# Squares off GpSimd, compress weights loaded early, and a few moves in the first stage of a one-core decoder layer

## The chip, the cores and the metric

The kernel runs on one core of a Trainium2 chip. The metric is the time of one execution in device microseconds (us); three runs of the kernel before gave 1188.03, 1190.80 and 1195.89 us, so the median is 1190.8 us. The engines are named as the profile names them: PE (matrix multiply), PEld (its weight load, which overlaps), DVE (vector), ACT (scalar activations), POOL (GpSimd) and SP (it only issues DMA here).

## The reference, cut to what matters

One transformer layer on 256 tokens of width 2048, in float32:

```python
h = rmsnorm(x, norm_attn)                  # y = x * rsqrt(mean(x*x) + eps) * g
proj = h @ w_in                            # columns split among three mixers
o_a = dilated_mixer(pA, tbl_a)             # three windows, weighted by softmax shares
o_b = moba_mixer(q, k, v, tbl_b)
o_c = nsa_mixer(q_c, kv_c, g_c, cmp_w1, cmp_w2, cmp_pe, tbl_c)
x = x + concatenate([o_a, o_b, o_c]) @ w_out
h = rmsnorm(x, norm_mlp)
x = x + conv_ffn(h, w_up, conv_w, conv_b, w_down)
return rmsnorm(x, norm_final)
```

Two pieces matter here. `rmsnorm` needs the sum of squares of each token over all 2048 features. `nsa_mixer` compresses blocks of 32 keys (and values) by a small two-layer network, `gelu(blocks @ cmp_w1) @ cmp_w2`, and weighs its three branches by gates `g_c`, a sigmoid of 36 projected columns.

## The kernel before, in words

**Layout.** Activations lie feature by feature: `x` is 16 tiles (kt = 0 to 15) of 128 features by 256 tokens. Every weight tile comes from HBM as float32 into one of four `raw` buffers (loads issued by SP, in program order while the first stage is written, L663). ACT rounds it into `wh` (L122) and DVE computes the rest `wl = raw - wh` (L124); there are five buffers of each. `x` is split in the same way into `xx` (ACT L174, DVE L175). A product is then two PE instructions: `wl` against the high part of `xx` (L186, 256 columns) and `wh` against both parts (L182, 512 columns). `Weights.get` runs three jobs ahead.

**First units.** `first_units` works on six units of 128 output columns (`ckv0` to `ckv5`) at once, while x arrives. Its blocks go by kt: four small ones for kt 0 and 1, two for kt 2 and 3, then three groups of three (kt 4 to 7, 8 to 11, 12 to 15); a block of a group is one load of 512 KB and 8 products, a group 24 products. After each piece of x lands, `x_load` splits it, and POOL squares it and adds the squares one tile at a time into `ssq` (L240, L242). `Rms` then sums `ssq` over the partitions by a matmul with ones (L146), which stands in PE's order among the products of the last group. `evac` scales the six units and writes the compressed branch's keys and values into `K2`.

**The group `c`, then the rest.** `tm_group("c")` multiplies 420 columns (L385 to L387, 96 matmuls), among them the gate columns. `compress` loads its 2 MB of weights `w1t` in four DMAs (L414), into the space that held the squares (`sqx`, tag `oo`), runs 32 matmuls of 49 columns (L422, two records each in the trace), a gelu, and three small matmuls with `w2t` (L445 to L447). At the end of the group the gates are turned end to end by a matmul with `flip` (L402). Then come the query units `cq0` to `cq5`, the other heads, all attention, and the output projection in two passes. The second pass (L701 to L710) adds to each tile of x, splits it again for the feed-forward part, and POOL squares and adds it (L168, L170) into `ssq2`; two units `up` of the feed-forward part are multiplied meanwhile, and the second norm's matmul (L146) stands in PE's order among them. The up and down projections, about 60% of the time, follow.

The order on PE, ACT, DVE and POOL is set when the kernel is built, by a scheduler that simulates the engines; only SP's order in the first units is the program's own.

Of the kernel before, what the change touches and what calls it, by code (L numbers as in the profile page):

```python
# [11 lines left out]
F32 = mybir.dt.float32  # L12
F32R = mybir.dt.float32r
AF = mybir.ActivationFunctionType
# [3 lines left out]
P = 128  # L18
S = 256
# [70 lines left out]
def trunk(ctx, tc, xT, wfm, wtm, wout, wup, wdown, w1, w2, pe, relT, convp, onehot, maskc, cmask, vbmask, out):  # L90
# [19 lines left out]
    def warm_sqrt(src):  # L110
        A.activation(warm, src, AF.Sqrt)

    warm_sqrt(ones[:, :1])

    def split_w(src, n, before=None):
        if before:
            before()
        raw = wp.tile([P, CHUNK], F32, name="raw", bufs=RAW_BUFS)
        dst = raw[:, :n]
        DMA(dst if len(src.shape) == 2 else dst.rearrange("p (u c) -> p u c", u=src.shape[1]), src)  # L120
        wh = wp.tile([P, CHUNK], F32R, name="wh")
        A.copy(wh[:, :n], raw[:, :n])  # L122
        wl = wp.tile([P, CHUNK], F32R, name="wl")
        V.tensor_tensor(wl[:, :n], raw[:, :n], wh[:, :n].bitcast(F32), ALU.subtract)  # L124
        return wh, wl
# [13 lines left out]
    class Rms:  # L139
# [17 lines left out]
        def spread(self, keep=True):  # L157
# [5 lines left out]
            rb = cp.tile([P, S], F32, name="rbc")  # L163
            V.tensor_copy(rb, ps[:, S:])
            return rb

    def add_squares(ssq, o, tmp):
        G.tensor_tensor(tmp, x[:, o, :], x[:, o, :], ALU.mult)  # L168
        if o:
            G.tensor_tensor(ssq, ssq, tmp, ALU.add)  # L170

    def split_x(gi, kts, xx):
        for kt in kts:
# [33 lines left out]
    with tc.tile_pool(name="sc", bufs=2, space=bass.MemoryType.PSUM) as scp, \  # L207
# [20 lines left out]
        order.insert(len(order) - 8, ("t", "b"))  # L228
        ssq = cp.tile([P, S], F32, name="ssq2")

        sqx = ap.tile([P, 12, S], F32, name="sqx", tag="oo")

        def x_load(*cuts):
            def go():
                for a, b in zip(cuts, cuts[1:]):
                    i, j = GX * (a > 0) + a * S, GX + b * S
                    DMA(gx[:, i:j], xT[:, i:j])
                    split_x(0, range(a, b), xx)
                    c = a % 12
                    G.tensor_tensor(sqx[:, c:c + b - a, :], x[:, a:b, :], x[:, a:b, :], ALU.mult)  # L240
                    for o in range(max(a, 1), b):
                        G.tensor_tensor(ssq, ssq if o > 1 else sqx[:, 0, :], sqx[:, o % 12, :], ALU.add)  # L242
            return go


# [3 lines left out]
            blocks += [(0, 2, 4 * g, 4, cuts), (2, 2, 4 * g, 4, None), (4, 2, 4 * g, 4, None)]  # L249
        for u, nu, kt, nk, cuts in blocks:  # L250
            src = wfm[u:u + nu, :, kt * P:(kt + nk) * P].rearrange("u p c -> p u c")
            jobs.append((src[:, 0, :] if nu == 1 else src, nu * nk * P, x_load(*cuts) if cuts else None))
        for kind, name in order:
            (fm_jobs if kind == "f" else tm_jobs)(name)
        for o in range(NK):
# [13 lines left out]


        flip = ap.tile([P, P], F32, name="flip")
        V.tensor_copy(flip, ident[:, ::-1])
        relt = ap.tile([NB, NB], F32, name="relt")
        G.dma_start(relt, relT)
        oneh = rp.tile([NB, 384], F32, name="sb")
# [13 lines left out]
        table = dr.tile([NB, 384], F32, name="table")  # L289

        def biases():
            ps = opp.tile([P, 512], F32, name="o")
            T.matmul(ps[:NB, :384], relt, oneh, start=True, stop=True)
            rs = ap.tile([NB, 384], F32, name="rs", tag="oo")
            V.scalar_tensor_tensor(rs, ps[:NB, :384], -1.0, mc, ALU.mult, ALU.add)
            G.dma_start(table, rs)

# [61 lines left out]
        def first_units():  # L359

            pss = [pool.tile([P, 512], F32, name=n) for pool, n in
                   ((mm, "mm"), (opp, "o"), (scp, "sc"), (scp, "sc"), (mm, "mm"), (ptp, "pt"))]
            for u, nu, kt, nk, _ in blocks:
                if (u, kt) == (0, 12):
                    clear()
                    n = Rms([ssq])
                w = wq.get()
                for j in range(nu):
                    products(pss[u + j], tuple(t[:, nk * P * j:nk * P * (j + 1)] for t in w), nk, kt, xx, kt == 0, kt == 12)
                    if kt == 12:  # L370
                        if u + j == 0:
                            norm(n)
                        evac(f"ckv{u + j}", pss[u + j])

        def tm_group(name):
            n = len(_TM[name])
            pss = [mm.tile([P, 512], F32, name="mm") for _ in range(2)]
            for c in range(8):
                wh, wl = wq.get()
                for i in range(2):  # L380
                    kt = 2 * c + i
                    a, b = wh[:, i * n:(i + 1) * n], wl[:, i * n:(i + 1) * n]
                    for tt in range(2):
                        ts = slice(tt * P, tt * P + P)
                        T.matmul(pss[tt][:, :n], xx[:, kt, 0, ts], a, start=kt == 0, stop=False)  # L385
                        T.matmul(pss[tt][:, :n], xx[:, kt, 1, ts], a, start=False, stop=False)  # L386
                        T.matmul(pss[tt][:, :n], xx[:, kt, 0, ts], b, start=False, stop=kt == NK - 1)  # L387
                yield
            nv = n - n % P
            v = vt[name] = ap.tile([P, 2, nv], F32, name=f"v_{name}", tag=f"v{name}")  # L390
            rt = st["rt"]
            if name == "c":
                ge = st["gate"] = ap.tile([P, 2, 36], F32, name="gate")
            for tt in range(2):
                A.activation(v[:, tt, :], pss[tt][:, :nv], AF.Copy, scale=rt[:, tt, 0:1])
                if name == "c":
                    A.activation(ge[:, tt, :], pss[tt][:, nv:n], AF.Exp, scale=rt[:, tt, 1:2])
            if name == "c":
                V.tensor_scalar_add(ge, ge, 1.0)
                V.reciprocal(ge, ge)  # L400
                ps = mm.tile([P, 512], F32, name="mm")
                T.matmul(ps[:, :72], flip, ge.rearrange("p t g -> p (t g)"), start=True, stop=True)  # L402
                V.tensor_copy(ge.rearrange("p t g -> p (t g)"), ps[:, :72])

        oparts = {}
        oo = []
# [2 lines left out]
        cmp = {}  # L409

        def compress():
            w1t = ap.tile([P, 4, 8 * P], F32, name="w1t", tag="oo")
            for i in range(4):
                DMA(w1t[:, i, :], w1[i // 2, :, i % 2 * 1024:i % 2 * 1024 + 1024])  # L414
                yield
            hps = ptp.tile([P, 512], F32, name="pt")
            for i in range(2):
                k2 = K2[i][:, :, 16:256].rearrange("p h (b l) -> p h b l", l=16)
# [40 lines left out]
            yield  # L459

        def cmp_attention():
            sm = rp.tile([P, 2, 12, 16], F32, name="sb")
            for tt in range(2):
                sps = scp.tile([P, 512], F32, name="sc")
# [194 lines left out]
        def drain():  # L659
            while side:  # L660
                step()

        with tc.manual_schedule(engines={mybir.EngineType.SP}):  # L663
            first_units()
        biases()
# [35 lines left out]
        for o in range(NK):  # L701
            if o % 2 == 0:
                w = wq.get()
            ps = mm.tile([P, 512], F32, name="mm")
            for i in range(4):
                a, b = (t[:, (o % 2 * 4 + i) * P:(o % 2 * 4 + i + 1) * P] for t in w)
                product_in_one(ps, a, b, oparts[6 + i], i == 0, i == 3)
            add_to_x(o, ps, 1)
            split_x(1, [o], xx)
            add_squares(ssq2, o, rp.tile([P, S], F32, name="sq", bufs=1) if o else ssq2)  # L710


    jobs = []
# [160 lines left out]
```

## Time and profile before

| | us |
|---|---|
| median of 3 runs | 1190.8 |
| the profiled execution | 1189.61 |
| its span in the trace | 1187.9 |
| PE busy in it | 1163.6 |
| DVE, ACT, POOL busy | 861.6, 671.3, 83.9 |

An engine's busy time says how much of the span it worked; what matters for the end is where PE, busy for nearly all of it, stood still or ran slowly, and which engine or transfer ended that. "PEclk" is the clock that PE was granted: 1.00 is the upper level of 2.4 GHz, 0.50 the lower of 1.2 GHz, and a stretch in between is a mean of both.

### The profile page before, as it was taken

The numbers are of one execution on the slowest core, as the hardware profiler recorded it, in microseconds if no ns is written. First come the engines' busy times: TensorE is split into PE (matmuls) and PEld (weight loads), VectorE is DVE, ScalarE is ACT, GpSimd is POOL, SyncE is SP. The second block draws the span as 40 slices with busy tenths as digits, with TensorE's granted clock in tenths as the row PEclk, the third lists the DMA queues.
The fourth block names the chain that finished last, engine by engine and source line by source line (L and its number), as shares of the span: only waits on it lengthen the run. The fifth ranks groups of instructions, "written<-read, shape, count | busy, mean of one in ns | idle before, by whom it ended". The sixth has DMA issues, their size and how long they took to land.

```text
span 1187.9 us, 18694 instructions
## 1 busy us (share of the span) xinstructions
PE 1163.6 (98%) x6874; PEld 1022.6 (86%) x6874; DVE 861.6 (73%) x1635; ACT 671.3 (57%) x1153; POOL 83.9 (7%) x105
## 2 busy tenths in 40 slices
PE   7999999999999999999999999999999999999996
PEld 6798888898888888888888888888888888888886
DVE  7857998767686797888888888888888655454453
ACT  6465697766774456565565565565565544444441
POOL 7400000100000190000000000000000000000000
PEclk9989999999999999999999999999999999999998
DMA  8565445566565645555555555555555656666661
GB/s 267 162 233 187 135 118 171 145 191 184 156 168 154 221 159 186 192 192 185 192 192 184 191 192 184 192 192 185 192 192 183 190 180 184 187 182 192 183 190 71
DMA packets 66795, 214.91 MB, mean 181 GB/s; under 512 B 7584, under 2 KB 10416, under 8 KB 66704
## 3 DMA queue, kind: packets, MB, share of 16 engines
q1 hardware_dynamic: 64896, 209.19, 55.2%
q0 software_dynamic: 1808, 4.53, 2.1%
q8 instruction: 54, 0.88, 0.3%
q14 instruction: 37, 0.30, 0.1%
HBM read 211.55 MB, written 2.15 MB: 180 GB/s over the span
## 4 chain that ended last, share of the span: by engine, by line
PE 91%; POOL 5%; DMA 2%; DVE 1%; issue 0%; ACT 0%; SPq 0%; DVEq 0%; POOLq 0%
PE up L182 40%; PE up L186 20%; PE mm L182 12%; PE mm L186 6%; PE mm L387 2%; PE mm L385 2%; PE mm L386 2%; PE o L580 1%; POOL ssq L242 1%; POOL ssq L170 1%; POOL sq L168 1%; PE sc L509 1%; DMA w1t<-in_w_dram 1%; DMA raw<-in_wfm_dram 1%; PE pt L422 1%; PE pt L560 1%
## 5 line engine op out<-in xcount | busy, mean ns | idle before, releaser
L124 DVE TENSOR_TENSOR wl<-raw,wh 128x1024 fp32r<-128x1024 f32 (+4 forms) x411 | 485.0, 1182 | 200.2 <-ACT wh L122 190.9
L122 ACT CAST wh<-raw 128x1024 fp32r<-128x1024 f32 (+4 forms) x411 | 411.1, 1001 | 290.2 <-PE up L182 192.7
L182 PE MATMUL up<-xx,wh 128*128 128x512 f32 x1408 | 485.2, 394 | 0.0
L186 PE MATMUL up<-xx,wl 128*128 128x256 f32 x1408 | 380.2, 280 | 0.0
L182 PEld LDWEIGHTS up<-xx,wh 128*128 128x128 f32 x1408 | 258.6, 188 | 51.2
L186 PEld LDWEIGHTS up<-xx,wl 128*128 128x128 f32 x1408 | 266.0, 189 | 7.9
L182 PE MATMUL up<-aa,wh 128*128 128x512 f32 x660 | 230.7, 393 | 0.0
L186 PE MATMUL up<-aa,wl 128*128 128x256 f32 x660 | 184.1, 283 | 0.0
L182 PE MATMUL mm<-xx,wh 128*128 128x512 f32 x448 | 162.6, 403 | 4.4 <-ACT wh L122 4.4
L182 PEld LDWEIGHTS up<-aa,wh 128*128 128x128 f32 x660 | 123.0, 188 | 27.3
L186 PE MATMUL mm<-xx,wl 128*128 128x256 f32 x448 | 125.2, 289 | 3.1 <-DVE wl L124 3.1
L186 PEld LDWEIGHTS up<-aa,wl 128*128 128x128 f32 x660 | 124.1, 188 | 1.4
L203 ACT COPY low<-up 128x256 f32<-128x256 f32 x88 | 32.7, 372 | 129.9 <-PE up L182 127.3
L182 PEld LDWEIGHTS mm<-xx,wh 128*128 128x128 f32 x448 | 84.8, 192 | 20.6 <-ACT wh L122 4.4
L186 PEld LDWEIGHTS mm<-xx,wl 128*128 128x128 f32 x448 | 86.5, 193 | 7.0 <-DVE wl L124 4.4
L204 DVE TENSOR_TENSOR low<-up,low 128x256 f32<-128x256 f32 x88 | 37.4, 424 | 57.0 <-ACT low L203 57.0
L182 PE MATMUL mm<-oo,wh 128*128 128x512 f32 x192 | 67.8, 399 | 0.0
L738 ACT ACTIVATE acc<-u,cw 128x256 f32<-128x256 f32 x88 | 53.3, 606 | 3.0 <-DVE u L736 0.6
L186 PE MATMUL mm<-oo,wl 128*128 128x256 f32 x192 | 51.7, 282 | 0.0
L385 PE MATMUL mm<-wh,xx 128*128 128x384 f32 (+2 forms) x128 | 46.3, 363 | 0.0
L387 PE MATMUL mm<-wl,xx 128*128 128x384 f32 (+2 forms) x128 | 46.0, 361 | 0.0
L386 PE MATMUL mm<-wh,xx 128*128 128x384 f32 (+2 forms) x128 | 45.9, 359 | 0.0
(206 smaller groups left out, 1259.0 us busy)
## 6 DMA issues: line engine op xcount, KB each, us to landing
raw<-in_wup_dram SPq DMA_DIRECT2D x176, 512.0 KB, 4.3
raw<-in_wdown_dram SPq DMA_DIRECT2D x80, 512.0 KB, 3.7
raw<-in_wfm_dram SPq DMA_DIRECT2D x62, 512.0 KB, 4.0
raw<-in_wo_dram SPq DMA_DIRECT2D x32, 384.0 KB, 3.1
raw<-in_wtm_dram SPq DMA_DIRECT2D x16, 384.0 KB, 3.4
bias<-table POOLq DMA_DIRECT2D x32, 128.0 KB, 3.7
raw<-in_wtm_dram SPq DMA_DIRECT2D x8, 512.0 KB, 4.1
raw<-in_wo_dram SPq DMA_DIRECT2D x8, 512.0 KB, 4.3
```

The costliest lines, as they stand in the source:

```text
L122: A.copy(wh[:, :n], raw[:, :n])
L124: V.tensor_tensor(wl[:, :n], raw[:, :n], wh[:, :n].bitcast(F32), ALU.subtract)
L168: G.tensor_tensor(tmp, x[:, o, :], x[:, o, :], ALU.mult)
L170: G.tensor_tensor(ssq, ssq, tmp, ALU.add)
L182: T.matmul(ps, a, m.rearrange("p c s -> p (c s)"), start=start, stop=stop)
L186: T.matmul(ps[:, :S], b, m[:, 0, :], start=False, stop=False)
L203: A.copy(t, ps[:, S:])
L204: V.tensor_tensor(t, ps[:, :S], t, ALU.add)
L385: T.matmul(pss[tt][:, :n], xx[:, kt, 0, ts], a, start=kt == 0, stop=False)
L386: T.matmul(pss[tt][:, :n], xx[:, kt, 1, ts], a, start=False, stop=False)
L387: T.matmul(pss[tt][:, :n], xx[:, kt, 0, ts], b, start=False, stop=kt == NK - 1)
L738: A.activation(acc, u[:, 2:], AF.Identity, bias=cw[:, n, 3:4], scale=cw[:, n, 0:1])
```

## The change

The squares of the first norm go to ACT: the first four tiles straight into a four-tile sum `acc`, later pairs into a rotating `k` buffer, which DVE adds to `acc`; two more DVE additions fold `acc` into `ssq`. The squares of the second norm go to ACT in pairs of tiles too, and DVE adds the pairs. The four loads of `w1t` are issued by SP among those of the first units and of the group `c`. The first four weight loads go into spare `p` buffers instead of `raw` ones, the very first of them issued by ACT. Six matmuls of ones on ones run at the start. The gates are turned in `cmp_attention`, where they are used, not at the end of the group. `rs` moves to a `p` buffer, since `oo` now holds `w1t`.

```diff
+    idle = mm.tile([P, 512], F32, name="mm")
+    for _ in range(6):
+        T.matmul(idle[:, :P], ones, ones, start=True, stop=True)
-    def split_w(src, n, before=None):
+    def split_w(src, n, before=None, raw=None, load=DMA):
...
-        raw = wp.tile([P, CHUNK], F32, name="raw", bufs=RAW_BUFS)
+        raw = wp.tile([P, CHUNK], F32, name="raw", bufs=RAW_BUFS) if raw is None else raw()
...
-    def add_squares(ssq, o, tmp):
-        G.tensor_tensor(tmp, x[:, o, :], x[:, o, :], ALU.mult)
-        if o:
-            G.tensor_tensor(ssq, ssq, tmp, ALU.add)
...
-        sqx = ap.tile([P, 12, S], F32, name="sqx", tag="oo")
+        acc = ap.tile([P, 4, S], F32, name="acc", tag="vb")
+        def squares(a, b):
+            if b <= 4:
+                A.activation(acc[:, a:b, :], x[:, a:b, :], AF.Square)
+                return
+            for o in range(a, b, 2):
+                sq = rp.tile([P, 2, S], F32, name="k", bufs=KEY_BUFS)
+                A.activation(sq, x[:, o:o + 2, :], AF.Square)
+                part = acc[:, o % 4:o % 4 + 2, :]
+                V.tensor_tensor(part, part, sq, ALU.add)
...
                     split_x(0, range(a, b), xx)
-                    c = a % 12
-                    G.tensor_tensor(sqx[:, c:c + b - a, :], x[:, a:b, :], x[:, a:b, :], ALU.mult)
-                    for o in range(max(a, 1), b):
-                        G.tensor_tensor(ssq, ssq if o > 1 else sqx[:, 0, :], sqx[:, o % 12, :], ALU.add)
...
+                        + ((lambda: rp.tile([P, 384], F32, name="p", bufs=6), A.dma_start if (u, kt) == (0, 0) else DMA) if kt < 2 else ()))
...
-            rs = ap.tile([NB, 384], F32, name="rs", tag="oo")
+            rs = rp.tile([NB, 384], F32, name="p", bufs=6)
...
                 if (u, kt) == (0, 12):
                     clear()
+                    squares(8, 12)
+                    squares(12, 16)
+                    V.tensor_tensor(acc[:, :2, :], acc[:, :2, :], acc[:, 2:, :], ALU.add)
+                    V.tensor_tensor(ssq, acc[:, 0, :], acc[:, 1, :], ALU.add)
                     n = Rms([ssq])
+                if u == 0 and kt in (4, 8):
+                    for o in range(kt - 4, kt, 2):
+                        squares(o, o + 2)
                 w = wq.get()
+                if u == 4 and kt > 2:
+                    i = kt // 4 - 1
+                    for j in ((0,), (1,), (2, 3))[i]:
+                        DMA(w1t[:, j, :], w1[j // 2, :, j % 2 * 1024:j % 2 * 1024 + 1024])
...
-                ps = mm.tile([P, 512], F32, name="mm")
-                T.matmul(ps[:, :72], flip, ge.rearrange("p t g -> p (t g)"), start=True, stop=True)
-                V.tensor_copy(ge.rearrange("p t g -> p (t g)"), ps[:, :72])
...
         def compress():
-            w1t = ap.tile([P, 4, 8 * P], F32, name="w1t", tag="oo")
-            for i in range(4):
-                DMA(w1t[:, i, :], w1[i // 2, :, i % 2 * 1024:i % 2 * 1024 + 1024])
-                yield
...
         def cmp_attention():
+            ge = st["gate"].rearrange("p t g -> p (t g)")
+            ps = ptp.tile([P, 512], F32, name="pt")
+            T.matmul(ps[:, :72], flip, ge, start=True, stop=True)
+            V.tensor_copy(ge, ps[:, :72])
...
             split_x(1, [o], xx)
-            add_squares(ssq2, o, rp.tile([P, S], F32, name="sq", bufs=1) if o else ssq2)
+            if o % 2 == 1:
+                sq = rp.tile([P, 2, S], F32, name="k", bufs=KEY_BUFS)
+                A.activation(sq, x[:, o - 1:o + 1, :], AF.Square)
+                if o == 1:
+                    acc = sq
+                else:
+                    V.tensor_tensor(acc, acc, sq, ALU.add)
+        V.tensor_tensor(ssq2, acc[:, 0, :], acc[:, 1, :], ALU.add)
```

**The order, first place: PE in and behind the group `c`.** The rows are instructions in PE's order: line, operation, result and operands, columns, and how many follow alike. Before, all narrow matmuls of `compress` (the two rows with `w1t`) stand together behind the last matmul of the group, with the gates' matmul behind them and then the first products of `cq0`:

```order
L387 MATMUL mm<-wl,xx 128x420
L422 MATMUL pt<-k_0_111,w1t 128x49 x16
L422 MATMUL pt<-k_1_112,w1t 128x49 x16
L402 MATMUL mm<-gate,flip 128x72
L182 MATMUL mm<-xx,wh 128x512
```

Now, with new line numbers (L402 to L404 are the group's three matmuls, L432 the narrow ones):

```order
L404 MATMUL mm<-wl,xx 128x420
L432 MATMUL pt<-k_0_117,w1t 128x49 x16
L402 MATMUL mm<-wh,xx 128x420
L403 MATMUL mm<-wh,xx 128x420
L404 MATMUL mm<-wl,xx 128x420
L402 MATMUL mm<-wh,xx 128x420
L403 MATMUL mm<-wh,xx 128x420
L404 MATMUL mm<-wl,xx 128x420
L432 MATMUL pt<-k_1_118,w1t 128x49 x16
L402 MATMUL mm<-wh,xx 128x420
```

The narrow matmuls are now two bursts inside the group, 41 of the group's matmuls ahead of the first, 6 between them and 49 behind. The three matmuls with `w2t` follow directly on the group's last one; before, they stood behind the whole of `cq0`. The gates' matmul moved to just ahead of the first scores of `cmp_attention`.

**Second place: DVE at the end of the first units.** Before (L124 is `wl`, L204 the first unit's evacuation, L148 the first step behind the norm's matmul):

```order
L175 SCALAR_TENSOR_TENSOR xx<-gx,xx 128x256 x4
L124 TENSOR_TENSOR wl<-raw,wh 128x1024 x3
L124 TENSOR_TENSOR wl<-raw,wh 128x840 x2
L204 TENSOR_TENSOR low<-mm,low 128x256
L124 TENSOR_TENSOR wl<-raw,wh 128x840
L148 TENSOR_SCALAR var<-mm 128x2
```

Now:

```order
L173 SCALAR_TENSOR_TENSOR xx<-gx,xx 128x256 x2
L240 TENSOR_TENSOR acc<-acc,k 128x512
L173 SCALAR_TENSOR_TENSOR xx<-gx,xx 128x256 x2
L240 TENSOR_TENSOR acc<-acc,k 128x512
L127 TENSOR_TENSOR wl<-raw,wh 128x1024
L374 TENSOR_TENSOR acc<-acc 128x512
L127 TENSOR_TENSOR wl<-raw,wh 128x1024
L375 TENSOR_TENSOR ssq_99<-acc 128x256
L127 TENSOR_TENSOR wl<-raw,wh 128x1024
L127 TENSOR_TENSOR wl<-raw,wh 128x840 x2
```

Two additions of pairs, one fold of 512 columns and one of 256 now stand among the last group's `wl`; the sum is complete behind the second of its three `wl`. On PE the matmul with ones moved five products forward, to just behind the first product of the last group's second block.

**Third place: SP in the first units.** Before, from the load of the last tiles of x on, the four `w1t` loads stand behind the group `c` and three loads for `cq0` and `cq1`. Now:

```order
L123 DMA raw<-in_wfm_dram 128x2x512 x2
L384 DMA w1t<-in_w_dram 128x1024
L123 DMA raw<-in_wfm_dram 128x2x512
L246 DMA gx<-in_xT_dram 128x512 x2
L123 DMA raw<-in_wfm_dram 128x2x512 x2
L384 DMA w1t<-in_w_dram 128x1024
L123 DMA raw<-in_wfm_dram 128x2x512
L123 DMA raw<-in_wtm_dram 128x840 x2
L384 DMA w1t<-in_w_dram 128x1024 x2
L123 DMA raw<-in_wtm_dram 128x840 x6
```

One load stands in the second group of three blocks, one in the third, and two behind the second load of the group `c`.

At the second norm, 80 matmuls of the `up` units stand on PE ahead of the matmul with ones, where there were 64. On DVE, 9 of the 1024-column `wl` lie between the first addition to x of the second pass and `ssq2`. The copy that makes `flip` is written at another place, but keeps its place in DVE's order. No further table load appears on ACT.

## Rows read from the trace of the kernel before

**Rows 1.** The page, part 1: busy us, share of the span, instructions.

```profile
PE 1163.6 (98%) x6874; PEld 1022.6 (86%) x6874; DVE 861.6 (73%) x1635; ACT 671.3 (57%) x1153; POOL 83.9 (7%) x105
```

**Rows 2.** Waits of PE, whole span: us in total, times, longest.

```profile
PE mm L182 <- ACT wh L122: 4.4, 1, 4.4
PE mm L186 <- DVE wl L124: 3.1, 3, 1.4
```

**Rows 3.** Timeline of PE, parts: start us, us, instruction, idle before and its releaser.

```profile
4.96 0.63 PE L182 MATMUL o<-xx,wh 128*128 128x512 f32 x1
...
9.48 0.40 PE L182 MATMUL mm<-xx,wh 128*128 128x512 f32 x1
...
18.55 0.38 PE L186 MATMUL mm<-xx,wl 128*128 128x256 f32 x1 [1.08 <-DVE wl L124]
...
43.28 0.80 PE L146 MATMUL mm<-ones,ssq 128*128 128x1 f32 x4 [1.80 <-POOL ssq L242]
...
68.78 1.90 PE L422 MATMUL pt<-k,w1t 128*128 128x49 f32 x16
71.12 8.05 PE L422 MATMUL pt<-k,w1t 128*128 128x49 f32 x48 [0.45 <-DMA w1t<-in_w_dram]
...
446.05 0.81 PE L146 MATMUL mm<-ones,ssq 128*128 128x1 f32 x4 [2.71 <-POOL ssq L170]
```

**Rows 4.** Windows: length; busy (instructions) PE, PEld, DVE, ACT, POOL; PEclk, DMA, GB/s.

```profile
15.00:20.00 5.00, 3.92 (x23) 3.23 (x22) 4.77 (x8) 2.81 (x4) 1.48 (x2) 1.00 0.89 299
20.00:35.00 15.00, 14.95 (x86) 12.89 (x86) 15.00 (x13) 9.20 (x14) 14.61 (x13) 1.00 0.74 240
43.28:47.00 3.72, 3.72 (x14) 3.33 (x15) 2.31 (x9) 1.09 (x2) 0.00 (x0) 0.54 0.87 290
68.80:79.20 10.40, 9.96 (x66) 9.66 (x65) 4.05 (x8) 7.98 (x16) 0.00 (x0) 0.76 0.86 335
79.20:84.60 5.40, 5.40 (x19) 4.69 (x20) 2.88 (x10) 1.35 (x5) 0.00 (x0) 0.51 0.55 187
412.00:443.00 31.00, 31.00 (x236) 29.67 (x234) 29.05 (x42) 18.19 (x27) 28.48 (x29) 1.00 0.53 174
446.00:449.70 3.70, 3.65 (x14) 3.26 (x15) 2.36 (x7) 2.81 (x4) 0.17 (x3) 0.54 0.66 202
```

**Rows 5.** DVE groups by form, 20 to 43 us: count, busy, mean ns, idle.

```profile
L124 DVE TENSOR_TENSOR wl<-raw,wh 128x1024 fp32r<-128x1024 f32 x7 | 12.3, 1800 | 0.2 <-ACT wh L122 0.2
L175 DVE SCALAR_TENSOR_TENSOR xx<-gx,xx 128x256 fp32r<-128x256 f32 x8 | 7.8, 1033 | 0.0
```

**Rows 6.** The same, 412 to 443 us.

```profile
L124 DVE TENSOR_TENSOR wl<-raw,wh 128x1024 fp32r<-128x1024 f32 x10 | 14.1, 1420 | 1.5 <-ACT wh L122 1.5
L175 DVE SCALAR_TENSOR_TENSOR xx<-gx,xx 128x256 fp32r<-128x256 f32 x16 | 10.9, 698 | 0.3 <-ACT xx L174 0.3
L687 DVE TENSOR_TENSOR gx<-mm,gx 128x256 f32<-128x256 f32 x16 | 6.6, 412 | 0.2 <-PE mm L193 0.2
```

**Rows 7.** The same, 480 to 1150 us, where POOL has no work.

```profile
L124 DVE TENSOR_TENSOR wl<-raw,wh 128x1024 fp32r<-128x1024 f32 x232 | 284.2, 1225 | 118.8 <-ACT wh L122 111.6
L740 DVE SCALAR_TENSOR_TENSOR acc<-u,cw,acc 128x256 f32<-128x256 f32 x82 | 39.8, 485 | 2.9
...
L124 DVE TENSOR_TENSOR wl<-raw,wh 128x512 fp32r<-128x512 f32 x15 | 10.4, 692 | 10.5 <-ACT wh L122 10.5
```

**Rows 8.** ACT groups by form, whole span.

```profile
L122 ACT CAST wh<-raw 128x512 fp32r<-128x512 f32 x17 | 10.5, 620 | 27.0 <-PE up L182 25.2 <-PE up L192 1.7
```

**Rows 9.** Timeline of ACT: the sixth unit's evacuation and the copy of the hidden layer.

```profile
73.05 0.36 ACT L203 COPY low<-pt 128x256 f32<-128x256 f32 x1
...
80.09 0.23 ACT L429 COPY hT<-pt 128x98 f32<-128x98 f32 x1
```

**Rows 10.** Timeline of DVE: the last step ahead of the `w2t` matmuls.

```profile
82.33 0.39 DVE L442 COPY hr<-hT 128x60 f32<-128x60 f32 x3
```

**Rows 11.** DMA issues, whole span: count, KB each, median us to landing.

```profile
w1t<-in_w_dram SPq DMA_DIRECT2D x4, 512.0 KB, 9.2
```

## What the change was predicted to do

> **What bounds the kernel now.** I read the page's busy times first, then PE's waits, its timeline around them, the windows for the granted clock, and only then the engines that PE waited for. PE is busy for 1163.6 of 1187.9 us [rows 1]; 24 us of the span are left. So the change can win in two ways only: where PE stands still, and where it works at the lower clock. Both happen at three places.
>
> At 43.28 us PE has waited 1.80 us for the first norm's sum, which POOL makes, and then works 3.72 us at a mean clock of 0.54 [rows 3, 4]. From 68.78 us the narrow matmuls of the compressed branch run together; PE waits 0.45 us for `w1t` between them, the granted clock falls to a mean of 0.76 for 10.4 us, and the first products behind them still run at 0.51 for 5.4 us [rows 3, 4]. At 446.05 us PE has waited 2.71 us for the second norm's sum, again POOL's, and then works 3.7 us at 0.54 [rows 3, 4].
>
> Two smaller losses lie at the start: 4.4 us until the first product, and three waits for `wl` of 3.1 us together, the longest 1.4, one of 1.08 at 18.55 us, so 0.6 for the third [rows 2, 3]. DVE, which makes `wl`, is busy in all of 20 to 35 us, while POOL is busy in 14.61 of the 15 [rows 4].
>
> **Part 1, the first norm.** POOL's squares and sums go; ACT gets 16 tiles of squares in 8 instructions, DVE six additions of 512 columns, one fold of 512 and one of 256. No square of 512 columns is shown; a copy of 512 takes 0.620 [rows 8], and I take that. A DVE two-operand instruction of 512 columns takes 0.692 [rows 7].
>
> Per group of three blocks PE needs 24 products at 0.35 us (86 matmuls fill 15 us, so 0.174 each [rows 4]): 8.4 us. DVE needs three `wl` and four splits of x. In 20 to 43 us these take 1.80 and 1.03 us [rows 5], so 9.5 us: more than PE. Where POOL has no work, `wl` takes 1.225, and the nearest three-operand instruction 0.485 [rows 7]; with two additions the group then costs 3 x 1.225 + 4 x 0.485 + 2 x 0.692 = 7.0 us. ACT has room too: 9.20 of 15 us busy [rows 4], and 1.24 us more per group. Both lie under PE, so DVE runs ahead through the last two groups, and the sum, complete behind the last group's second `wl`, is there when PE asks.
>
> Here a rule is weighed. The row shows DVE 1.5 to 2 times slower while POOL works; it doesn't show that POOL is the reason, since the DMA is busy at that time as well. At 412 to 443 us additions whose one operand lies in PSUM take 0.412 beside a busy POOL, while the splits take 0.698 [rows 6]: only instructions with two SBUF operands suffer. The Trainium skill ("SBUF — State Buffer", "Who interferes with whom") says that DVE and GpSimd share one pair of SBUF ports under an exclusive lock, the loser waiting for a whole instruction. By it the clean prices apply and the group costs 7.0 us; without it 9.5 plus two slow additions, some 11.5, and this part turns into a loss (a rival below).
>
> What goes: the wait of 1.80; the slow stretch behind it, 3.72 x 0.46 = 1.7; the third `wl` wait, 0.6. Of the wait of 1.08 I take half, 0.5: its `wl` comes faster, but its weights come in a stretch where the DMA was 0.89 busy [rows 4]. **4.6 us.** Bounds: 2, if the extra transfers slow the blocks, to 7, if the loads that no longer wait for `raw` buffers bring the 1.4, the other half of the 1.08 and some 0.5 ahead of the first product.
>
> **Part 2, the first loads and the six matmuls.** The first products run at 0.63 us where 0.40 is usual later [rows 3], so up to 2.4 us (six products from 4.96 to 9.48 us, 0.75 each instead of 0.35) could come from a faster clock there. I count nothing: the longest `wl` wait lies directly behind these products, its blocks wait for transfers, and whatever PE wins ahead of it is waited for there. The six run in PE's first 4.4 us, which are empty [rows 2]. Below nothing: a second idle stretch at the start could cost one slow stretch, 1.7.
>
> **Part 3, `w1t` and the narrow matmuls.** Four loads of 512 KB move from behind the group `c` into it and into the first units. PE's wait of 0.45 goes. At the lower clock 10.4 x 0.24 = 2.5 and 5.4 x 0.49 = 2.6 us are lost: together 5.5 us to win. The bursts now take 2 x 1.90 = 3.8 us each [rows 3], with six wide matmuls between. Before, a mean of 0.76 over 10.4 us means 5.0 at the lower level of 0.5, so the clock held through the first 5.4 us of narrow work, and either burst alone is shorter than that; but the wait of 1.80 at 43 us, shorter still, made it fall too. Bounds 0 and 5.5; I leave one slow stretch of the usual size, 1.7 us, and take **3.8 us**.
>
> The three `w2t` matmuls now stand right behind the group. From the end of the second burst 49 wide matmuls remain, at 0.174 or more each [rows 4] at least 8.5 us; the chain to them (copy of the hidden layer, gelu, copies) took 80.09 to 82.7, 2.6 us [rows 9, 10]. A table load and four key copies now stand in it, but it may take three times as long. I count no wait.
>
> The loads pass SP's queue, some 0.4 us for each issue, and every later load stands behind them. 20 to 35 us moved 240 GB/s at a DMA share of 0.74 [rows 4]. Per group x, three blocks and one `w1t` piece are 2.62 MB. At the lowest rate of a full stretch, 299 GB/s [rows 4], that is 8.8 us against PE's 8.4: 0.4 late twice, which the lead covers.
>
> The same page of the Trainium skill (its table in "A bandwidth-pool intuition that's wrong") gives about 358 GB/s from HBM; by it the group takes 7.3 us and the rival of late weights has nothing to stand on. The 299 GB/s came at a share of 0.89 [rows 4], 336 for a full one, still under it, so I go by the row and keep that rival.
>
> **Part 4, the second norm.** ACT gets 8 squares of 512, 5.0 us beside 18.19 of 31 busy [rows 4]. DVE in this stretch: 16 x 0.412 + 16 x 0.485 + 9 x 1.225 + 7 x 0.692 + 0.41 = 30.6 us, where 14.1 + 10.9 + 6.6 = 31.6 stand now with ten `wl` [rows 6]; so the sum is there at about 412 + 31 = 443. PE came to it at 446.05 - 2.71 = 443.3 [rows 3], and 16 more matmuls now stand ahead of it, 2.8 us: no wait. 2.71 and 3.7 x 0.46 = 1.7 go: **4.4 us**, bounds 2 and 4.8. The gates' matmul and its copy: nothing, PE only moves it.
>
> **The sum.** 4.6 + 3.8 + 4.4 = 12.8 us. Behind each place PE has no waits until the end, so the gain is kept. The profiled execution took 1189.6, so 1176.8; the median of the runs stands 1.2 above it: **1178 us**.
>
> **The rivals.**
> - *All of it:* the clock holds and the deeper queue brings blocks earlier: 7 + 5.5 + 4.4 = 16.9, 1174 us. For it: both bursts are shorter than 5.4 us.
> - *A new wait:* the `w2t` matmuls. The hidden layer's copy now stands on ACT behind the sixth unit's evacuation, which came at 73.05 [rows 9]. On the same count the group now ends at 68.8 + 7.6 = 76.4. If the evacuation stays so late, a chain of twice the 2.6 us ends at 78.3, one of three times at 80.9: a wait of 1.9 to 4.5, and a slow stretch of 1.7 behind it. I take 5 us back, 1183 us. Against it: three casts and the gates' work left ACT's queue ahead of it.
> - *Half the gain:* the clock falls in both bursts and the blocks are paced by DMA: 2 + 1 + 4.4, 1183 us.
> - *DVE is not freed:* the slow rows are not POOL's doing. Then eight slower additions, 6 us, stand on a full DVE: the first part gives -2.5, the fourth nothing; 1189 us.
> - *Slower:* late weights. A `w1t` load took 9.2 us to land with three others behind it [rows 11], and weights behind one in SP's queue land after it. If PE waits that long in both groups, 18.4 us, with a slow stretch each, 3.4, minus the 12.8: 1200 us. It decides once the stalls exceed 12.8. Against it: share 0.74.
>
> **How the numbers follow.** A change of 1% is 11.9 us, about what a measurement of this kernel tells from none, so under 1178.9 counts as faster. The forecast gets 0.44, its own range 1175 to 1181 (0.28 of it on the faster side); all of it 0.22; new wait 0.13; half the gain 0.12; DVE not freed 0.05; slower 0.04. Faster 0.28 + 0.22 = 0.50, same 0.46, slower 0.04. The range 1172 to 1186 leaves out the last two cases and a little of the second.
>
> **What would show it.** `wl` at 1.2 and the splits under 0.6 us at 20 to 40 us; no wait of PE at either matmul with ones; clock 1.00 around both; first units done near 44 us instead of 49. Waits of PE for casts in 20 to 45 us would show late weights, one at the first `w2t` matmul the new wait. A clock under 1.00 around 55 to 70 us shows how much of part 3 is left.

## The result, and the profile after

| | before | after |
|---|---|---|
| median (4 runs each, beside each other) | 1193.35 us | 1173.85 us |
| lowest, highest | 1188.03, 1195.89 | 1172.54, 1174.83 |
| profiled execution, its span | 1189.61, 1187.9 | 1172.54, 1170.8 |

The ratio is 0.9842 [0.98, 0.9883]: faster by 1.6%, with 1173.85 us where 1178 had been forecast. Three larger sets of the kernel before, timed later beside the experiments, have medians of 1190.18 (16 runs), 1190.73 (12) and 1190.42 (7); against those the gain is some 16.5 us, or 1.4%. The rest of this section reads the two profiled executions, whose spans differ by 17.1 us. The page's first part for the kernel after:

```profile
PE 1157.0 (99%) x6886; PEld 1018.9 (87%) x6886; DVE 851.4 (73%) x1651; ACT 677.8 (58%) x1169; POOL 23.8 (2%) x51
```

Against [rows 1], POOL's 83.9 us are down to 23.8. DVE, which took over all the additions, is busy 10.2 us less than before, because its other instructions became shorter. Waits of PE (us in total, times, longest), the four largest:

```profile
PE mm L163 <- DVE rtok L158: 1.3, 1, 1.3
PE mm L184 <- DVE wl L127: 1.1, 2, 0.6
PE mm L116 <- DVE ones L100: 1.1, 1, 1.1
PE mm L180 <- ACT wh L125: 0.9, 1, 0.9
```

The first lies in the last norm and was there before (1.3 us). The 4.4 us ahead of the first product are now split by the six matmuls of ones, and the waits for `wl` are 1.1 us, not 3.1 [rows 2]. No wait for `ssq` or `w1t` is left. PE's timeline at the places of [rows 3]:

```profile
4.87 0.80 PE L180 MATMUL mm<-xx,wh 128*128 128x512 f32 x1 [0.90 <-ACT wh L125]
...
9.10 0.63 PE L180 MATMUL mm<-xx,wh 128*128 128x512 f32 x1
...
12.09 0.39 PE L184 MATMUL mm<-xx,wl 128*128 128x256 f32 x1 [0.53 <-DVE wl L127]
...
17.12 0.38 PE L184 MATMUL mm<-xx,wl 128*128 128x256 f32 x1 [0.59 <-DVE wl L127]
...
37.00 0.50 PE L149 MATMUL mm<-ones,ssq 128*128 128x1 f32 x4
...
43.11 0.35 PE L402 MATMUL mm<-wh,xx 128*128 128x420 f32 x1
...
52.12 3.69 PE L432 MATMUL pt<-k,w1t 128*128 128x49 f32 x32
...
69.68 0.32 PE L455 MATMUL pt<-hT,w2t 128*128 128x51 f32 x2
...
433.95 0.50 PE L149 MATMUL mm<-ones,ssq 128*128 128x1 f32 x4
```

Both matmuls with ones stand without a bracket: PE waited for neither. The group `c` begins at 43.11 us, where it began at 48.88 before. At 69.68 us the `w2t` matmuls start without a wait. Windows of the kernel after (columns as in [rows 4]):

```profile
20.00:35.00 15.00, 15.00 (x88) 13.20 (x87) 11.85 (x19) 9.82 (x14) 0.00 (x0) 1.00 0.89 307
37.00:41.00 4.00, 4.00 (x26) 3.58 (x25) 2.32 (x9) 1.75 (x4) 0.00 (x0) 1.00 1.03 416
52.00:61.00 9.00, 9.00 (x76) 8.96 (x75) 6.11 (x11) 6.81 (x17) 2.13 (x4) 1.00 0.77 234
60.00:92.00 32.00, 32.00 (x182) 28.91 (x182) 22.73 (x44) 20.87 (x36) 0.00 (x0) 1.00 0.53 171
433.00:440.00 7.00, 7.00 (x44) 6.20 (x43) 5.68 (x10) 4.74 (x6) 0.00 (x0) 1.00 0.59 190
```

The granted clock is 1.00, the upper level of 2.4 GHz, in each: behind the first norm, through both bursts of narrow matmuls, behind them, and behind the second norm. These are the stretches that stood at 0.54, 0.76, 0.51 and 0.54 [rows 4]. DVE's groups by form, 20 to 43 us and then 395 to 428 us:

```profile
L127 DVE TENSOR_TENSOR wl<-raw,wh 128x1024 fp32r<-128x1024 f32 x6 | 7.3, 1220 | 3.2 <-ACT wh L125 3.2
L173 DVE SCALAR_TENSOR_TENSOR xx<-gx,xx 128x256 fp32r<-128x256 f32 x7 | 3.1, 478 | 0.0
L240 DVE TENSOR_TENSOR acc<-acc,k 128x512 f32<-128x512 f32 x4 | 2.7, 684 | 0.0
```

```profile
L127 DVE TENSOR_TENSOR wl<-raw,wh 128x1024 fp32r<-128x1024 f32 x12 | 14.6, 1222 | 2.3 <-ACT wh L125 2.1
L702 DVE TENSOR_TENSOR gx<-mm,gx 128x256 f32<-128x256 f32 x18 | 7.5, 417 | 0.2 <-PE mm L191 0.2
L173 DVE SCALAR_TENSOR_TENSOR xx<-gx,xx 128x256 fp32r<-128x256 f32 x16 | 7.0, 476 | 0.0
```

`wl` takes 1.22 us where it took 1.80 and 1.42, the split 0.48 where it took 1.03 and 0.70; the additions with a PSUM operand stay at 0.42 [rows 5, 6]. Two rows of DVE's timeline give the slack that is left:

```profile
34.44 0.42 DVE L375 TENSOR_TENSOR ssq<-acc 128x256 f32<-128x256 f32 x1
...
65.48 0.40 DVE L452 COPY hr<-hT 128x60 f32<-128x60 f32 x3
```

The sum is there at 34.86 us, 2.1 ahead of PE; the copies for `w2t` end at 65.9, 3.8 ahead.

**Where the 17.1 us came from.** Up to the group `c`: 48.88 - 43.11 = 5.8. From there to PE's arrival at the second norm, taking the wait of 2.71 and the 16 matmuls that now stand ahead (2.8 us) out: (443.34 - 48.88) - (431.15 - 43.11) = 6.4. The rest, 4.9, lies at and behind the second norm.

### The profile page after: what moved, and what is told of

The parts are those of the page before. It is cut to its first block, busy times and chain, and to the rows that moved or that the text cites. A ratio compares the mean times of both kernels' runs of the same rounds, so it can differ in the third digit from the quotient of the medians.

```text
span 1170.8 us, 18695 instructions
## 1 busy us (share of the span) xinstructions
PE 1157.0 (99%) x6886; PEld 1018.9 (87%) x6886; DVE 851.4 (73%) x1651; ACT 677.8 (58%) x1169; POOL 23.8 (2%) x51
## 4 chain that ended last, share of the span: by engine, by line
PE 98%; DMA 1%; DVE 1%; ACT 0%; SPq 0%; issue 0%; DVEq 0%
PE up L180 41%; PE up L184 21%; PE mm L180 13%; PE mm L184 6%; PE mm L404 2%; PE mm L402 2%; PE mm L403 2%; PE o L594 2%; PE sc L523 1%; PE mm L191 1%; PE mm L189 1%; PE mm L190 1%; DMA gx<-in_xT_dram 1%; PE pt L432 1%; PE pt L574 1%; PE sc L521 1%
## 5 line engine op out<-in xcount | busy, mean ns | idle before, releaser
L127 DVE TENSOR_TENSOR wl<-raw,wh 128x1024 fp32r<-128x1024 f32 (+3 forms) x407 | 474.2, 1166 | 197.7 <-ACT wh L125 188.5
L125 ACT CAST wh<-raw 128x1024 fp32r<-128x1024 f32 (+3 forms) x407 | 408.5, 1005 | 276.9 <-PE up L180 195.6
L180 PE MATMUL mm<-xx,wh 128*128 128x512 f32 x448 | 160.0, 398 | 0.9 <-ACT wh L125 0.9
L180 PEld LDWEIGHTS mm<-xx,wh 128*128 128x128 f32 x448 | 83.3, 189 | 17.1 <-ACT wh L125 1.2
L402 PE MATMUL mm<-wh,xx 128*128 128x384 f32 (+2 forms) x128 | 46.4, 364 | 0.0
L404 PE MATMUL mm<-wl,xx 128*128 128x384 f32 (+2 forms) x128 | 45.9, 360 | 0.0
```

Source lines behind the costliest of these rows:

```text
L180: T.matmul(ps, a, m.rearrange("p c s -> p (c s)"), start=start, stop=stop)
```

## The experiments

Every kernel here was timed beside the kernel before. Where a median is set against the changed kernel's, that is 1173.85 us, taken at another time.

**1. Who slows DVE?** Two kernels that put work back on POOL beside the changed kernel. The first squares and adds x there again, at both norms, into a scratch that nobody reads:

```diff
...
                     split_x(0, range(a, b), xx)
+                    for o in range(a, b):
+                        G.tensor_tensor(scr[:, o % 2, :], x[:, o, :], x[:, o, :], ALU.mult)
+                        if o:
+                            G.tensor_tensor(scs, scs if o > 1 else scr[:, 0, :], scr[:, o % 2, :], ALU.add)
...
             split_x(1, [o], xx)
+            G.tensor_tensor(scr[:, o % 2, :], x[:, o, :], x[:, o, :], ALU.mult)
+            G.tensor_tensor(scs, scs, scr[:, o % 2, :], ALU.add)
...
```

> The changed kernel, in which POOL squares and adds x once more beside ACT and DVE, into buffers that nobody reads (31 instructions at each norm, as before the change). Theory (POOL's SBUF operands slow DVE): wl rises from 1.22 to about 1.8 us and the splits from 0.44 to about 1.0 us between 20 and 40 us, DVE needs some 11 us for a group where PE needs 8.4, the first matmul of the group c moves from 43.1 to 47 to 50 us, and PE waits for the second norm's sum too: 1179 to 1187 us. Rival (DVE was slow because the DMA was busy, and only the wait for POOL's own sum was lost): DVE's rows stay at 1.22 and 0.44, the first matmul of the group stays within 1 us of 43.1, 1174 us.

Measured 1185.4 us, ratio to before 0.9943 [0.9924, 0.9963]; the group `c` starts at 50.57 us. The second fills a scratch with zeros at the first norm, which reads nothing:

```diff
...
                     split_x(0, range(a, b), xx)
+                    for o in range(2 * (b - a)):
+                        G.memset(scr, 0.0)
...
```

> The changed kernel with 32 memsets of 768 columns on POOL while x is loaded; POOL is about as busy between 5 and 35 us as before the change, but reads nothing from SBUF. If DVE suffers only from a POOL instruction that reads SBUF: wl 1.22, splits 0.44, first matmul of the group c at 43 us, 1174 us. Rival (any work of POOL on SBUF slows DVE): as with POOL's squares, wl near 1.8, first matmul at 46 us or later, 1177 us or more.

Measured 1175.13 us (two executions), 0.9865 [0.9824, 0.9906]; the group starts at 43.64. DVE's groups in 20 to 43 us, with the squares on POOL and then with the fills:

```profile
L127 DVE TENSOR_TENSOR wl<-raw,wh 128x1024 fp32r<-128x1024 f32 x8 | 12.3, 1570 | 0.0
L173 DVE SCALAR_TENSOR_TENSOR xx<-gx,xx 128x256 fp32r<-128x256 f32 x8 | 6.9, 895 | 0.0
L240 DVE TENSOR_TENSOR acc<-acc,k 128x512 f32<-128x512 f32 x4 | 4.8, 1192 | 0.0
```

```profile
L127 DVE TENSOR_TENSOR wl<-raw,wh 128x1024 fp32r<-128x1024 f32 x6 | 7.3, 1221 | 3.9 <-ACT wh L125 3.9
L173 DVE SCALAR_TENSOR_TENSOR xx<-gx,xx 128x256 fp32r<-128x256 f32 x8 | 3.5, 482 | 0.0
```

The windows of 20 to 35 us of the two:

```profile
20.00:35.00 15.00, 13.76 (x69) 11.79 (x70) 15.00 (x13) 7.89 (x13) 14.69 (x12) 0.89 0.68 222
```

```profile
20.00:35.00 15.00, 15.00 (x88) 13.22 (x88) 11.12 (x18) 9.37 (x15) 11.39 (x16) 1.00 0.85 303
```

POOL is busy in both, 14.69 and 11.39 of 15 us; DVE slows only beside the instructions that read SBUF, and it does so while the DMA moves less (222 GB/s, against 303 beside the fast DVE). So the slow rows are POOL's doing, neither the DMA's nor mere activity on POOL. With the squares back, PE waits 6.9 us for `wl`, and the median is 11.5 us above the changed kernel's, though nobody waits for those squares:

```profile
PE mm L184 <- DVE wl L127: 6.9, 4, 3.7
```

**2. Each norm alone.** The kernel before with only the first norm's squares moved (the diff ahead, its `squares`, the folds and the place of `Rms`; loads, ones, gates and the second norm as before):

> The kernel before with the first norm's squares on ACT and DVE and nothing else. Theory (DVE freed and the sum in time are worth most of the first units' gain): the first matmul of the group c moves from 48.9 to 43.5 to 45 us, no slow stretch there, 4 to 5.5 us gained. Rival (the deeper load queue and the six matmuls made the first units faster): it stays at 46.5 us or later, 2.5 us gained or less. The narrow matmuls and the second norm lose what they lose now.

And with only the second norm's:

```diff
-            add_squares(ssq2, o, rp.tile([P, S], F32, name="sq", bufs=1) if o else ssq2)
+            if o % 2 == 1:
+                sq = rp.tile([P, 2, S], F32, name="k", bufs=KEY_BUFS)
+                A.activation(sq, x[:, o - 1:o + 1, :], AF.Square)
+                if o == 1:
+                    acc = sq
+                else:
+                    V.tensor_tensor(acc, acc, sq, ALU.add)
+        V.tensor_tensor(ssq2, acc[:, 0, :], acc[:, 1, :], ALU.add)
```

> The kernel before with the second norm's change alone: its squares on ACT in pairs, the pairs added by DVE. Theory: PE's wait of 2.71 us at the second norm's matmul and the slow stretch of 1.7 us behind it go, 4.4 us in all, since splits and additions on DVE return to about 0.48 and 0.42 us; the first units stay as before (group c's first matmul near 48.9 us). Ratio to before about 0.996. Rival: DVE with the additions becomes the bound there, PE waits for DVE instead of POOL at the same matmul, gain under 1 us, ratio 0.999 or more.

The first: 1186.53 us, 0.9965 [0.9947, 0.9983]. The second: 1184.05 us, 0.9947 [0.9929, 0.9964]. PE's timeline of the first, then its window over the compressed branch:

```profile
43.22 0.35 PE L398 MATMUL mm<-wh,xx 128*128 128x420 f32 x1
...
64.90 11.46 PE L435 MATMUL pt<-k,w1t 128*128 128x49 f32 x64 [1.65 <-DMA w1t<-in_w_dram]
...
443.40 1.01 PE L146 MATMUL mm<-ones,ssq 128*128 128x1 f32 x4 [2.70 <-POOL ssq L170]
```

```profile
60.00:92.00 32.00, 30.35 (x160) 27.79 (x159) 16.47 (x38) 16.59 (x34) 0.18 (x1) 0.79 0.54 189
```

The group `c` starts at 43.22, as early as with the whole change (43.11), which is 5.7 us earlier than before. The median gained 3.7 us; its interval, 2.1 to 6.3, still holds 5.7. In the profiled execution, one of the slower ones (1188.81, of 1182.04 to 1189.29), the loads of `w1t` are issued 4.3 us earlier (58.03, not 62.29), less than PE gained, so PE waits 1.65 us for them where it waited 0.45. The clock averages 0.79 over the 32 us; but the kernels with the old branch scatter there by themselves, with 0.84 and 0.79 in two profiles of the kernel before and 0.89 with the second norm alone. So about 1.2 us of part 1 go to the later wait in this profile; that part 1 needs part 3 for its whole price is not shown by the medians. Of the second kernel, the matmul with ones and the window around it:

```profile
444.25 0.50 PE L146 MATMUL mm<-ones,ssq 128*128 128x1 f32 x4
```

```profile
440.00:460.00 20.00, 20.00 (x120) 17.70 (x119) 13.03 (x24) 11.25 (x15) 0.17 (x3) 1.00 0.60 197
```

No wait, no slow stretch; the rival of a DVE that becomes the bound is out. Its median gained 6.7 us and its profiled execution 6.4, more than the 4.4 forecast: 1.6 us of the 6.4 are the clock over 60 to 92 us (0.89, not 0.84), where this kernel changes nothing.

**3. Early `w1t`, or narrow matmuls apart?** The changed kernel with its early loads, but the narrow matmuls together behind the group (`compress` yields four times before its first step):

> The changed kernel, all of it, but with the 32 narrow matmuls together behind the group c as before; their weights are still loaded early. Theory (the length of the narrow stretch lets the clock fall): no wait for w1t, but the granted clock falls some 5 us into the narrow matmuls and stays at the lower level into the first products of cq0, 4 to 5.5 us lost, 1178 to 1179.5 us. Rival (the clock fell because PE also waited for the load): clock 1.00 throughout, 1174 us.

Measured 1177.66 us, 0.9892 [0.9859, 0.9925]. Then the loads back in `compress`. The first attempt missed: without the tile that had held them back, SP issued all four at 7 us, ahead of the first units' weights, so it shows something else than was asked.

> The changed kernel with the four loads of w1t behind the group c, where they were before. Theory: all but one of the narrow matmuls stand together behind the group again, PE waits for w1t (between 0.5 and 3 us, since the group starts 5.8 us earlier) and the granted clock falls in and behind them; the loss is 5 to 8 us, time 1179 to 1182. Rival: the early loads are worth nothing by themselves because the first units' gain alone carried the result; then the time is 1173 to 1176.

1179.61 us, 0.9912 [0.9884, 0.994]: PE waits for `wl` four times, 4.0 us, and the group starts at 45.73; one early block of 2 MB costs the first units 2.6 us against the changed kernel's profile, where four loads are spread among them (in other profiles with these spread loads the group starts between 43.44 and 44.37). The second attempt puts `rs` back into the space of `w1t`, and the loads behind it:

```diff
...
-            rs = rp.tile([NB, 384], F32, name="p", bufs=6)
+            rs = ap.tile([NB, 384], F32, name="rs", tag="oo")
...
-                if u == 4 and kt > 2:
-                    i = kt // 4 - 1
-                    for j in ((0,), (1,), (2, 3))[i]:
-                        DMA(w1t[:, j, :], w1[j // 2, :, j % 2 * 1024:j % 2 * 1024 + 1024])
...
+            w1t = ap.tile([P, 4, 8 * P], F32, name="w1t", tag="oo")
+            for i in range(4):
+                DMA(w1t[:, i, :], w1[i // 2, :, i % 2 * 1024:i % 2 * 1024 + 1024])
+                yield
...
-        w1t = ap.tile([P, 4, 8 * P], F32, name="w1t", tag="oo")
...
```

> The changed kernel with the four w1t loads back in the compressed branch's own code, in the space that the bias table's tile frees late, so that they stand on SP behind the loads of group c and four more (the run e8 put them ahead of the first units' weights instead, and so did not answer this). Theory: first units as in the changed kernel (group c from 43.1 to 44 us), the narrow matmuls together behind the group, PE waits 1 to 2 us for w1t and the granted clock falls there for 10 us or more; loss 5 to 8 us, time 1179 to 1182. Rival: the early loads are worth only the wait; time 1175 to 1176.

Measured 1179.23 us, 0.9905 [0.9889, 0.9922]. PE's timeline of the narrow matmuls, in the changed kernel and then together behind the group:

```profile
52.12 3.69 PE L432 MATMUL pt<-k,w1t 128*128 128x49 f32 x32
...
56.85 3.69 PE L432 MATMUL pt<-k,w1t 128*128 128x49 f32 x32
```

```profile
63.79 9.37 PE L434 MATMUL pt<-k,w1t 128*128 128x49 f32 x64
```

The windows over the branch, with the matmuls together and loads early, then with the loads late:

```profile
60.00:92.00 32.00, 32.00 (x188) 29.43 (x187) 19.27 (x40) 18.17 (x35) 0.00 (x0) 0.89 0.46 157
```

```profile
60.00:92.00 32.00, 31.55 (x175) 28.87 (x174) 18.69 (x40) 18.88 (x38) 0.34 (x1) 0.84 0.59 204
```

Of the first, (1 - 0.89) x 32 = 3.5 us are lost to the clock with no wait at all, and its median is 3.8 above the changed kernel's. Of the second, 5.1 to the clock and 0.45 to the wait; its median is 5.4 above. So most of part 3 is the splitting of the narrow matmuls, which the early loads make possible; the wait itself is the small piece. How the 5.4 divides beyond that stays open, since the runs of the two kernels overlap (1176.93 to 1179.67 and 1178.61 to 1181.35).

**4. The ones and the spare buffers.** The changed kernel without the six matmuls of ones:

> The changed kernel without the six matmuls of ones at the start. Theory: nothing is lost, since the first products run at about 0.63 us to 9.5 us with them as without; group c's first matmul stays near 43.1 us, time 1173 to 1175. Rival: the six matmuls keep the clock up somewhere in the first 20 us; without them the first full-speed product comes later than 9.5 us, group c's first matmul at 45 us, time 1175.5 to 1177.

1173.93 us, 0.9865 [0.9837, 0.9892], group `c` at 43.44: no gain from the ones shows. With ones, but the first loads in `raw` buffers again, all issued by SP:

> The changed kernel with its first four weight loads in the usual raw buffers, all issued by SP. Theory: a product or two comes up to 1.4 us later before 20 us (the waits for wl at 13 and 18.5 us of 1.42 and 1.08 return), but the last groups take it up, so that group c starts within 1 us of 43.1 and the time is 1173.5 to 1175. Rival: the deeper queue is what carries the 1.5 us of the first units above the forecast; then group c starts at 44.6 or later and the time is 1175.5 or more.

1175.06 us, 0.987 [0.9844, 0.9896], group `c` at 45.00. I took the ones for the cause, since the first products ran at 0.40 us in that trace, and took both away:

> The changed kernel without the matmuls of ones and with the first loads in the raw buffers, so neither half of that part of the change. Theory from e7: there the ones made the first products fast, PE then waited 2.50 us at 13.29, the clock fell behind that wait and 1.9 us were lost at group c. Without the ones the first products run at 0.63 us, the wait is 1.7 us or less, no fall, and group c starts at 43.1 to 43.6; time 1173 to 1174.5. Rival: the raw buffers themselves are late; group c starts at 45 us again, time 1175 or more.

1174.47 us, 0.9867 [0.9853, 0.9882]. My theory fell; PE's timeline and the window:

```profile
13.27 0.39 PE L184 MATMUL mm<-xx,wl 128*128 128x256 f32 x1 [2.63 <-DVE wl L127]
...
44.98 0.35 PE L402 MATMUL mm<-wh,xx 128*128 128x420 f32 x1
```

```profile
5.00:20.00 15.00, 12.37 (x54) 10.21 (x55) 10.56 (x19) 11.24 (x20) 1.92 (x3) 0.89 0.98 318
```

Here PE goes on at 13.27 us, not 12.09, after a wait of 2.63 us instead of 0.53, and behind that the clock falls: 0.11 x 15 = 1.7 us. So in both profiles without the spare buffers the group starts 1.9 us later, nearly all of it the clock. That the buffers are the cause is not shown. With them that product comes anywhere from 12.09 to 13.36 us (13.36 with the matmuls together, experiment 3), and the kernel of experiment 2 with the old loads went on at 13.04 after 1.67 us, kept its clock and started the group at 43.22. What differs in these two is that the first products reach the upper clock earlier, at 4.83 and 8.51 us against 9.59 there, and the block comes 0.2 us later, so that PE stands before it for longer. The medians lie 1.2 and 0.6 us above the changed kernel's, with overlapping runs. Last, eight ones with the spare buffers, which close the gap of 0.90 us:

> The changed kernel with eight matmuls of ones, so that the idle 0.90 us between them and the first product closes. Theory: the first products run at 0.40 us instead of 0.63, PE gains 2.4 us up to 9.5 us and gives them back in the wait for wl near 12 us (0.53 grows to 2.5 or more), group c starts at 43 us or, if the clock falls behind the longer wait, at 45; time 1173.5 to 1175.5. Rival: the gain stays, group c starts at 41.5, time 1171.5 to 1172.5.

1175.11 us, 0.9869 [0.9853, 0.9885]. Two rows of PE:

```profile
5.13 0.39 PE L180 MATMUL o<-xx,wh 128*128 128x512 f32 x1
```

```profile
12.89 0.39 PE L184 MATMUL mm<-xx,wl 128*128 128x256 f32 x1 [2.19 <-DVE wl L127]
```

The first products run at the upper clock, and PE gives all of it back in the wait (the group starts at 43.87), as part 2 had argued. No variant beats the changed kernel; the one without ones equals it. The moves of the gates' matmul and of `rs` were not tried alone.

**5. The spread of the kernel before.** One more profile of it, of an execution of 1196.13 us:

> The kernel before once more, for a second trace of it: its times spread over 8 us where those of the changed kernel spread over 2.3. If the spread is the clock's, PE's waits (1.80, 0.45 and 2.71 us) stand where they stood, and the length of the stretches at the lower clock behind them, or further such stretches elsewhere, account for the difference of the two spans to within 0.5 us. If it is not the clock's, the waits differ.

Its windows around the three places, then those of the first profile:

```profile
41.00:53.00 12.00, 8.74 (x33) 7.68 (x33) 5.12 (x12) 2.88 (x4) 3.17 (x3) 0.72 0.58 178
60.00:92.00 32.00, 31.16 (x157) 28.94 (x156) 18.42 (x34) 19.96 (x38) 2.15 (x4) 0.79 0.63 211
440.00:460.00 20.00, 17.05 (x82) 14.75 (x81) 11.28 (x16) 8.67 (x11) 10.15 (x13) 0.83 0.51 166
```

```profile
41.00:53.00 12.00, 10.20 (x51) 9.15 (x50) 7.47 (x16) 3.79 (x7) 2.14 (x2) 0.86 0.65 198
60.00:92.00 32.00, 31.55 (x173) 29.28 (x172) 19.46 (x40) 20.59 (x40) 2.15 (x4) 0.84 0.68 229
440.00:460.00 20.00, 17.29 (x92) 14.98 (x92) 10.92 (x17) 8.82 (x11) 5.78 (x9) 0.91 0.57 185
```

The span is 6.5 us longer. The clock takes (0.14 x 12) + (0.05 x 32) + (0.08 x 20) = 4.9 of it. The expectation held only in part: PE's waits did not stand still either, the one for the first norm was 3.26 us, not 1.80, and all together grew by 1.2.

## Why the prediction was right, and where it was too small

The mechanism was the one forecast at all three places; two sizes were too small. So the time lies below the forecast's own range (1175 to 1181) and is that of the rival "all of it" (1174, chance 0.22). Of its two reasons the clock held; the other, a deeper queue that brings blocks earlier, was not needed for it: with the kernel before's queue the group `c` began at 43.22.

- **Part 1** (4.6; measured 5.8). Prices were right: 1.22, 0.48 and 0.68 for the 1.225, 0.485 and 0.692 taken; a square of 512 columns 0.62, as taken. Wait, slow stretch and third `wl` wait (0.58, at 36.36 us) went. Too small was what the short waits give: the part counts 1.1, the third one and "of the wait of 1.08 I take half, 0.5". In the changed kernel the 1.08 became 0.59, as taken; but the 1.42 at 13 us became 0.53, and a wait of 0.58 for a cast at 6.6 us that I did not list went, while the first product starts 0.5 later (4.87, not 4.36): 2.0 in all. With the first norm alone, 1.08 became 0.22 and the one at 6.6 us went, while 1.42 grew to 1.67: 1.8. That places 0.9 of the 1.2 by which the changed kernel exceeds the 4.6, and 0.7 of the 1.1 with the first norm alone; the rest I can't place.
- **The rule on the shared port pair.** By the Trainium skill ("SBUF — State Buffer", "Who interferes with whom") DVE and GpSimd share one pair of SBUF ports, and on this the clean prices were taken; the squares and fills on POOL agree, 0.90 against 0.48 us for the split. The same page of the Trainium skill counts two-input instructions of DVE against GpSimd operations that read SBUF, not against those that only write it, and the fills (0.48) show that limit too.
- **Part 2** (0). Right for the ones. What the spare buffers are worth stays open: with them the group starts at 43.11, with the old loads at 43.22 in one kernel and at 45.00 and 44.98 in two others. The part's most, 2.4 us from a faster clock, was read too large: 0.58 of the time from 4.96 to 9.48 us was the wait for the cast at 6.6 us.
- **Part 3** (3.8; 5.4 by the medians of experiment 3). Too small is the step "I leave one slow stretch of the usual size, 1.7 us": none was left, 1.00 from 52 to 92 us. The full 5.5, which the part had worked out, was the right term; no row of before shows such bursts, so the 1.7 was a guess between its bounds of 0 and 5.5. Of the 6.4 us in the spans 0.9 I can't place.
- **Part 4** (4.4; 4.9 in the spans, 6.7 in the median of experiment 2, whose interval is 0.36 to 0.71% or 4.3 to 8.5 us). The wait and the slow stretch went, as forecast.
- **Rivals.** *A new wait:* the copies came 3.8 us ahead of the `w2t` matmuls. *Late weights:* 307 GB/s in 20 to 35 us, and the only waits of PE for weights behind 4.87 us are 0.53 and 0.59, ahead of the first `w1t` load's issue at 17.52; the early block of experiment 3, 2.6 us, shows what badly placed loads cost. *DVE is not freed:* out by experiment 1.

The median before lay higher beside the changed kernel (1193.35) than in the three runs shown (1190.8): four runs that scatter by 8 us. So some 2.5 of the 19.5 us between the two medians are luck. In experiment 5 most of such a difference is the clock's (4.9 of 6.5 us). The changed kernel's four runs fall into 1172.5 to 1173.0 at a mean clock of 0.997 and 1174.7 to 1174.8 at 0.995: with most of its slow stretches, most of its scatter is gone.

## What to carry to other kernels

Price a POOL instruction that reads SBUF by what it adds to each two-operand instruction of DVE beside it, not by its own time, and look for it even where nobody waits for POOL. A short wait of PE can cost about twice its length when the clock falls behind it (1.80 us cost 3.5 here), and narrow matmuls can cost the clock too (3.5 us here, with no wait): split them among wide ones, and load their weights early enough that this is possible, but spread. An earlier group can run into the next late load (1.65 us of wait with the first norm alone, where 0.45 stood before).

## What the runs showed of the hardware

- What POOL adds to DVE is nearer to a fixed piece for each instruction than to a factor: with the squares back, 0.35 us on a `wl` of 1.22, 0.42 on a split of 0.48, 0.51 on an addition of 0.68; before, 0.58 and 0.56 on the first two at the first norm, and 0.20 and 0.22 at the second [rows 5, 6]. What sets the size of the piece stays open.
- 32 narrow matmuls of 49 columns in two bursts of 3.69 us, 1.0 us of wide matmuls between, kept the clock at 1.00; the same work in one piece of 9.37 us (with the loads early) did not.
- The length of a wait alone does not tell whether the clock falls behind it: it fell behind 1.80, 2.50, 2.63 and 2.71 us, and did not behind 1.42, 1.67, 2.02 (fills on POOL) and 2.19.
- The DMA moved 416 GB/s over 4 us at a share of 1.03 (37 to 41 us), more than the 336 that I had worked out for a full share; with the early block of `w1t` it moved 373 over 5 to 20 us at 1.02. Both are above the 358 GB/s that the prediction weighed against its row, so here the measurement decides.
- In some profiles (squares on POOL, fills on POOL, the second attempt at late loads, eight ones) the clock falls once more in 106 to 122 us, to a mean of 0.89, 1.8 us; in the changed kernel's profile it does not. What sets this off stays open.
